# A decoder trunk whose first FFN takes x times the norm's weights, with the root put on its results, and whose last two column halves end in banks of their own

## The chip, the cores and the metric

The kernel runs on one core of one Trainium2 chip. The metric is the device time of one execution in microseconds, as the median of several runs. In profile lines PE is TensorE's matmuls, PEld its weight loads, DVE is VectorE, ACT is ScalarE, POOL is GpSimd and SP is SyncE, on whose queue nearly all DMAs are issued.

## The reference, cut to what matters

```
def rms_norm(x, g):
    y = x * rsqrt(mean(x * x, axis=-1) + 1e-6)
    return y * g

def swiglu(x, w_in, w_out):
    gate, up = split(x @ w_in, 2, axis=-1)
    return (silu(gate) * up) @ w_out

h = x                                           # (1, 256, 1024) float32
for layer in range(2):
    h = h + 0.5 * swiglu(rms_norm(h, ffn1_norm[layer]), ffn1_w_in[layer], ffn1_w_out[layer])   # 1024 -> 2 * 2816 -> 1024
    hn = rms_norm(h, mix_norm[layer])
    h = h + attention(hn)                       # layer 0: stick-breaking; layer 1: sliding window with sinks, shared K/V
    h = h + 0.5 * swiglu(rms_norm(h, ffn2_norm[layer]), ffn2_w_in[layer], ffn2_w_out[layer])
    # after layer 0: the shared K and V are computed from rms_norm(h, kv_norm) @ kv_w
return rms_norm(h, final_norm)
```

## The kernel before, in words

All 256 tokens are held in two tiles of 128 (t is 0 or 1); `hN` holds the stream, by tile and by halves of 512 columns (j is 0 or 1). Weights stream from HBM once, in pieces of 1 MB into five buffers `raw`. For accuracy each product is made of three: a weight is split into `w_hi` (cast on ACT, L362) and `w_lo` (difference on DVE, L364), the operand into `xh` and `xl` (both in the tile `xT`), and `step` does hi times hi, lo times hi and hi times lo into one PSUM bank, 512 columns wide.

An FFN (`ffn`) goes through its 2816 columns in blocks. The first block is `plain` (gate columns, then up columns), the second is `narrow` (256 columns of each), and four blocks are `strassen`: seven products instead of eight, with sums of operands (`operand_sums`, tiles `S_h` and `S_l`) and sums of weights (DVE, and DMAs that add, issued by POOL). `silu` and `mul` make `m` from gate and up, `turn` transposes it on PE (L579) and splits it into `aT_h` and `aT_l`, and `out` multiplies it with `w_out` into four banks, the accumulators of tile and half (`accs`). These banks hold, before the first `out`, the transposed operand, out of which `operand_sums` takes its differences; so the first output product has to wait until those have been read.

**The opening.** x comes in four DMAs of 256 KB (tile, half), the first weight in four DMAs of 256 KB (`cut` 4), all on SP's queue. The norm's 1024 weights come in as a tile of 128 by 8 (`gcols`); DVE spreads them over a diagonal (`diag`) and PE multiplies this with ones, so that every partition has all weights in two banks (`g0`). Per tile ACT squares the two halves with their sums (`sq`, L438), DVE adds them up (L442), POOL takes the power of -0.5 (L445, the root), DVE scales x by root and weights (`xs`, L468), PE transposes (L413), ACT casts (L419) and DVE subtracts (L420) into `xT`. PE meanwhile does 40 products of constants ("warm"), which have the lowest priority.

**The order of the work.** The program is a list of tasks, each with an engine, an estimated duration, a priority (the position `plan.pos` in PE's dense work, less a lead) and the buffers that it reads and writes. `Plan.order` simulates the engines with these estimates and issues the tasks in the order that comes out; on the chip each engine then runs its list in order. A changed estimate can so change the order on any engine.

**The sliding-window stage** (`sliding_window`, its inner function `heads`) handles eight pairs of heads. For each: scores (PE, `kT_s,qT`), row maxima (DVE, L1140), the exponentials with their sums (ACT, L1149 and L1156), the inverse and the scaling of `e` (DVE, L1163 to L1166), six transposes of `e` (PE, L1174), two copies `ws` out of PSUM (ACT, and DVE at L1180), and the product with the values (PE, `ws,v_s`). Between these PE does query steps (`w_hi,xT`, 256 wide, with the rotary operations `qr_t` and `qr` on DVE) and steps of the output projection (`w_hi,o_h`).

**The end.** The last FFN has `ending` set: its last products go tile by tile and half by half, and the very last step (t = 1, j = 1) is done in two groups of three products of 256 columns into the two halves of one bank. `last` adds the results to the stream (L1304), squares (ACT L1309, DVE L1312), adds up (L1319), takes the root (POOL L1321), multiplies with the last norm's weights (L1325) and scales: columns 0 to 640 on DVE (L1331), 640 to 1024 on ACT (L1334), each followed by its output DMA (L1336).

Of the kernel before, what the change touches and what calls it, by code (L numbers as in the profile page):

```python
# [53 lines left out]
MASK_FROM = 2  # L54
QORD = (('q', 0, 1), ('q', 0, 0), ('q', 1, 0), ('q', 2, 0), ('h', 0, 0), ('h', 0, 1), ('q', 1, 1), ('h', 1, 0), ('h', 1, 1), ('q', 2, 1), ('h', 2, 0), ('q', 3, 0), ('h', 2, 1), ('q', 3, 1), ('h', 3, 0), ('h', 3, 1))
# [111 lines left out]
def dve(n):  # L167
    return n / 0.96 + 70
# [11 lines left out]
def kernel(  # L180
# [76 lines left out]
    one = pool.tile([P, 1], F32, name="one")  # L257
# [63 lines left out]
    def dma(src, dst, nbytes, w, prio, r=()):  # L321
        T("SP", nbytes / (300.0 if prio < -8e5 else PLAIN), lambda: nc.sync.dma_start(out=dst(), in_=src), r=r, w=w, prio=prio)
# [164 lines left out]
    def operand_sums(accs):  # L487
# [16 lines left out]
        T("ACT", act(512), lambda: ACT.copy(out=s[1].ap, in_=a[1][0].ap), r=B(a[1][0]), w=B(s[1]))  # L504
# [36 lines left out]
    def ffn(w_in, w_out, acc, rest, finish, kv=None, blocks=BLOCKS, first=False, ending=False):  # L541
        wi, wo = by_k(w_in), by_k(w_out)
        ring = [banks[i] for i in rest[0:3]]
# [3 lines left out]
        outs = {}  # L547
# [8 lines left out]
        def make_sums():  # L556
            nonlocal SH, SL
            SH, SL = operand_sums(accs)
# [4 lines left out]
        def col(h, i, c, n=512):  # L563
            return wi[:, 4 * i:4 * i + 4, h * DFF + c:h * DFF + c + n]

        def silu(dst, src, r, w, n=512):
            T("ACT", act(n), lambda: ACT.activation(out=dst(), in_=src(), func=AF.Silu), r=r + [(consts, "tbl")], w=w)

        def mul(dst, a_, b_, r, w, n=512):
            T("DVE", dve(n), lambda: DVE.tensor_mul(out=dst(), in0=a_(), in1=b_()), r=r, w=w, lat=LAT["DVE"] + TM)  # L570
# [17 lines left out]
        def plain(n, c, by_t, cut=2):  # L588
# [15 lines left out]
            def after_gate(t, bank):  # L604
                ms[t] = m = STG.get([P, 512], F32, "m")
                silu(lambda: m.ap, lambda: bank.ap, B(bank), B(m))

            def after_up(t, bank):
                m = ms[t]
                mul(lambda: m.ap, lambda: m.ap, lambda: bank.ap, B(bank), B(m))  # L610
                turn(m, t, aT)
# [30 lines left out]
        def narrow(n, c, by_t):  # L642
# [5 lines left out]
            def part(t, i):  # L648
# [5 lines left out]
                if i == 1:  # L654
                    m = STG.get([P, 512], F32, "m")
                    silu(lambda: m.ap[:, 0:256], lambda: bs[t].ap[:, 0:256], B(bs[t]), B(m), 256)
                    mul(lambda: m.ap[:, 0:256], lambda: m.ap[:, 0:256], lambda: bs[t].ap[:, 256:512], B(bs[t]), B(m), 256)
                    turn(m, t, aT, 2)
# [5 lines left out]
        def strassen(n, c, between):  # L664
# [13 lines left out]
            def mul_less(dst, a_, b_, r, w):  # L678
                T("DVE", dve(512), lambda: DVE.scalar_tensor_tensor(out=dst(), in0=b_(), scalar=-1.0, in1=a_(), op0=ALU.mult, op1=ALU.mult),
                  r=r, w=w, lat=LAT["DVE"] + TM)  # L680
# [21 lines left out]
            silu(lambda: s1.ap, lambda: s1.ap, [], B(s1))  # L702
# [4 lines left out]
            mul_less(lambda: s1.ap, lambda: s1.ap, lambda: u2.ap, B(u2), B(s1))  # L707
# [9 lines left out]
            silu(lambda: m.ap, lambda: a.ap, B(a), B(m))  # L717
            mul_less(lambda: m.ap, lambda: m.ap, lambda: p5.ap, B(p5), B(m))
# [11 lines left out]
        def out_step(n, i, kk, w, t, j, cut=False):  # L730
            if cut:

                for c in range(2):
                    (sh, sl), keys = of_a(outs[n][0], t, 2 * i + kk)
                    hi, lo = w
                    bank, now = accs[t][j], slice(256 * c, 256 * c + 256)

                    def run(now=now, cols=slice(512 * j + 256 * c, 512 * j + 256 * c + 256)):
                        mm(bank.ap[:, now], sh(), hi.ap[:, kk, cols], False, False)
                        mm(bank.ap[:, now], sl(), hi.ap[:, kk, cols], False, False)  # L740
                        mm(bank.ap[:, now], sh(), lo.ap[:, kk, cols], False, True)
                    dense(3 * mmr(256), run, r=[(hi, kk), (lo, kk)] + keys + (B(bank) if c else []), w=[(bank, c)])
                return
# [36 lines left out]
        for t in range(NT):  # L780
            for js in ((0,), (1,)) if ending else ((0, 1),):
                for n, i, w in ends:
                    for kk in range(2):
                        for j in js:
                            if ending and t == js[-1] == kk == 1 and (n, i) == ends[-1][0:2]:
                                out_step(n, i, kk, w, t, j, True)
                            else:
# [264 lines left out]
    def sliding_window(w_q, w_o, p0, others_, finish):  # L1052
# [54 lines left out]
        def heads(g, i):  # L1107
# [29 lines left out]
            T("PE", 850 if ready else 1230, scores, r=[(qT, (g, t)) for t in range(NT)] + [(kT_s, t) for t in range(NT)] + MWIN, w=B(*z))  # L1137
# [29 lines left out]
            T("DVE", 300 + dve(512) + dve(256), inverse, r=[(SM, (n, par, t)) for par in range(2) for t in range(NT)] + [(ES, (n, par)) for par in range(2)],  # L1167
# [8 lines left out]
            T("PE", 620, turns, r=[(e, (par, t)) for par in range(2) for t in range(NT)] + ID, w=B(*z))  # L1176
# [13 lines left out]
            T("PE", 800, av, r=[(w, k) for k in range(2)] + [(v_s, t) for t in range(NT)], w=[(o, k) for k in range(i, 2)])  # L1190
# [189 lines left out]
```

## Time and profile before

| | |
|---|---|
| time, median of 3 runs | 921.87 us (921.62 to 922.02) |
| the profiled execution: time, span | 922.51 us, 920.7 us |
| mean granted TensorE clock | 0.998 |
| busy: PE, DVE, ACT, POOL | 910.0, 797.9, 613.0, 55.7 us |
| first dense product of the first FFN | starts at 12.42 us |
| last product | ends at 913.98 us |
| mean HBM traffic | 226 GB/s |

The profile is of one execution, which took 0.64 us more than the median of the runs. The span runs from the first to the last instruction, and 1.8 us lie around it. A busy PE is one whose matmuls are under way; matmuls are pipelined, so that one of 512 columns shows some 0.39 us while the next starts after 0.23.

### The profile page before, as it was taken

The page shows a single profiled execution, that of the slowest core. Times are in us where ns is not written, and L with a number is a line of the kernel's source. Part 1 is how long each engine was busy: PE and PEld are TensorE (multiplying, and loading weights), DVE is VectorE, ACT ScalarE, POOL GpSimd, SP SyncE. Part 2 cuts the span into 40 slices and gives each one's busy share as a digit, 9 for nine tenths or more (in the row PEclk, how much of TensorE's full clock was granted, in tenths as well). Part 3 has the DMA queues.
Part 4 walks back from the last instruction along what each step waited for, and adds up shares of the span by engine and source line. Part 5 has one row for each costly group of instructions (what it writes and reads, how often), then busy time and mean ns, then how long its engine had stood idle before and what let it go on. Part 6 is the DMA issues. An engine that isn't in the chain of part 4 may idle for free.

```text
span 920.7 us, 11926 instructions
## 1 busy us (share of the span) xinstructions
PE 910.0 (99%) x4499; PEld 753.2 (82%) x4499; DVE 797.9 (87%) x962; ACT 613.0 (67%) x870; POOL 55.7 (6%) x65
## 2 busy tenths in 40 slices
PE   9999999999999999999999999999999999999997
PEld 6888888888888888888888888888897788888885
DVE  7979998798876887999879789998788798799984
ACT  6657667577887647676656477676758575667662
POOL 1010101010000000010000001010000000011000
PEclk9999999999999999999999999999999999999999
DMA  9878999895943577999884579999853358699961
GB/s 313 317 181 247 287 282 252 291 230 157 309 163 126 162 216 197 250 290 288 261 311 184 160 189 266 303 281 260 270 169 116 92 172 239 187 243 303 277 201 46
DMA packets 101930, 209.19 MB, mean 227 GB/s; under 512 B 3952, under 2 KB 24944, under 8 KB 101872
## 3 DMA queue, kind: packets, MB, share of 16 engines
q1 hardware_dynamic: 83104, 171.53, 53.0%
q0 software_dynamic: 18480, 36.70, 23.9%
q8 instruction: 35, 0.57, 0.2%
q10 hardware_dynamic: 288, 0.20, 0.1%
q14 instruction: 23, 0.19, 0.1%
HBM read 207.37 MB, written 1.05 MB: 226 GB/s over the span
## 4 chain that ended last, share of the span: by engine, by line
PE 97%; DVE 1%; ACT 1%; DMA 0%; issue 0%; DVEq 0%; ACTq 0%
PE ps L240 93%; PE ps L579 2%; PE ps L413 1%; PE ps L1174 1%; ACT e L1149 0%; DMA gcols<-in_ffn_norm_dram 0%; DVE w_lo L364 0%; DVE e L1166 0%; PE ps L1099 0%; ACT xT L419 0%; DVE small L1140 0%; DVE hN L1304 0%; DVE diag L1238 0%; DVE xT L420 0%; DVE hg L1325 0%
## 5 line engine op out<-in xcount | busy, mean ns | idle before, releaser
L364 DVE TENSOR_TENSOR w_lo<-raw,w_hi 128x1024 fp32r<-128x1024 f32 x418 | 491.2, 1218 | 32.0 <-ACT w_hi L362 30.8
L362 ACT CAST w_hi<-raw 128x1024 fp32r<-128x1024 f32 x418 | 417.3, 1051 | 99.7 <-PE ps L240 57.9
L240 PE MATMUL ps<-w_hi,xT 128*128 128x512 f32 (+1 forms) x920 | 270.6, 378 | 0.0
L240 PEld LDWEIGHTS ps<-w_hi,xT 128*128 128x128 f32 x920 | 166.9, 188 | 30.3
L240 PE MATMUL ps<-w_lo,xT 128*128 128x512 f32 (+1 forms) x460 | 172.5, 375 | 0.0
L240 PE MATMUL ps<-w_hi,aT_h 128*128 128x512 f32 x353 | 140.5, 398 | 0.0
L240 PE MATMUL ps<-w_lo,aT_h 128*128 128x512 f32 x353 | 137.7, 390 | 0.0
L240 PE MATMUL ps<-w_hi,aT_l 128*128 128x512 f32 x353 | 137.3, 389 | 0.0
L240 PE MATMUL ps<-w_hi,S_h 128*128 128x512 f32 x272 | 106.6, 392 | 0.0
L240 PE MATMUL ps<-w_lo,S_h 128*128 128x512 f32 x272 | 106.0, 390 | 0.0
L240 PE MATMUL ps<-w_hi,S_l 128*128 128x512 f32 x272 | 105.9, 389 | 0.0
L240 PEld LDWEIGHTS ps<-w_lo,xT 128*128 128x128 f32 x460 | 86.6, 188 | 15.8
L524 DVE TENSOR_TENSOR raw<-raw 128x1024 f32<-128x1024 f32 x66 | 78.6, 1218 | 0.3
L240 PEld LDWEIGHTS ps<-w_lo,aT_h 128*128 128x128 f32 x353 | 66.2, 188 | 14.2
L240 PEld LDWEIGHTS ps<-w_hi,aT_l 128*128 128x128 f32 x353 | 66.4, 188 | 12.8
L240 PEld LDWEIGHTS ps<-w_hi,aT_h 128*128 128x128 f32 x353 | 66.3, 188 | 12.6
L529 POOL DMA_DIRECT2D raw<-in_ffn_w_in_dram x32 | 41.0, 1282 | 526.5 <-ACT w_hi L362 285.6
L240 PEld LDWEIGHTS ps<-w_lo,S_h 128*128 128x128 f32 x272 | 51.1, 188 | 10.7
L240 PEld LDWEIGHTS ps<-w_hi,S_h 128*128 128x128 f32 x272 | 51.1, 188 | 10.3
L240 PEld LDWEIGHTS ps<-w_hi,S_l 128*128 128x128 f32 x272 | 51.1, 188 | 10.3
L419 ACT CAST aT_h<-ps 128x512 fp32r<-128x512 f32 (+1 forms) x48 | 26.4, 550 | 47.1 <-PE ps L579 47.1
L240 PE MATMUL ps<-xT,w_hi 128*128 128x512 f32 (+1 forms) x136 | 47.2, 394 | 0.1
(168 smaller groups left out, 900.8 us busy)
## 6 DMA issues: line engine op xcount, KB each, us to landing
raw<-in_ffn_w_in_dram SPq DMA_DIRECT2D x76, 1024.0 KB, 7.6
raw<-in_ffn_w_out_dram SPq DMA_DIRECT2D x44, 1024.0 KB, 5.5
raw<-in_ffn_w_in_dram POOLq DMA_DIRECT2D x32, 1024.0 KB, 9.4
raw<-in_sb_w_qkv_dram SPq DMA_DIRECT2D x12, 1024.0 KB, 7.7
raw<-in_ffn_w_in_dram SPq DMA_DIRECT2D x16, 512.0 KB, 5.2
raw<-in_ffn_w_in_dram SPq DMA_DIRECT2D x16, 256.0 KB, 5.3
raw<-in_sb_w_o_dram SPq DMA_DIRECT2D x4, 1024.0 KB, 6.8
raw<-in_swa_w_q_dram SPq DMA_DIRECT2D x4, 1024.0 KB, 8.7
```

The lines of the kernel that those rows point to most:

```text
L240: PE.matmul(ps, lhsT=lhsT, rhs=rhs, start=start, stop=stop, skip_group_check=True)
L362: T("ACT", act(m), lambda sl=sl: ACT.copy(out=flat(hi)[:, sl], in_=flat(raw)[:, sl]), r=[(raw, i) for i in rs] + first, w=[(hi, i) for i i ...
L364: T("DVE", dve(m), lambda sl=sl: DVE.tensor_sub(out=flat(lo)[:, sl], in0=flat(raw)[:, sl], in1=flat(hi)[:, sl].bitcast(F32)), r=[(raw, i) ...
L413: PE.transpose(out=bank.ap[:, i * P:(i + 1) * P], in_=s, identity=ident)
L419: T("ACT", act(n), lambda: ACT.copy(out=hi[2](), in_=src()), r=B(bank), w=[hi[0:2]])
L524: T("DVE", dve(m), lambda sl=sl: DVE.tensor_add(out=flat(dst)[:, sl], in0=flat(dst)[:, sl], in1=flat(src)[:, sl]), r=[(src, k) for k in ks ...
L529: T("POOL", 1500, lambda: nc.gpsimd.dma_start(out=dst.ap, in_=src, accum_op=ALU.add), w=[(dst, 0), (dst, 1)], prio=plan.pos - LOADS, lat=5 ...
L579: PE.transpose(out=tr.ap[:, i * P:(i + 1) * P], in_=m.ap[:, i * P:(i + 1) * P], identity=ident)
L1174: PE.matmul(z[par].ap[:, i_ * P:(i_ + 1) * P], lhsT=e.ap[:, par * 384 + c:par * 384 + c + P], rhs=ident, start=i_ == 0, stop=True, is_tran ...
```

## The change

*First FFN.* x is no longer scaled before its transposes. `first_operand` transposes x itself, taking every fourth column of a half for one transpose, so that the norm's weights lie per partition and column of the transposes; DVE multiplies the bank with them in place; cast and subtraction follow. For this the rows of `w_in` are grouped as (half, partition, 4) (`wi4`), in all blocks of this FFN. The weights come in as 128 by 2 by 4, and `diag`, `one` and `g0` are gone. The root and its negative (`roots`) are put onto the results: as the scale of `silu` and as the scalar of `mul` and `mul_less`. The sums of operands now begin after the first SiLU (`WAITM`). The second tile's x is issued behind four pieces of the first weight instead of two (`X1`).

*Planned costs.* The estimates for DMAs at the opening and for four kinds of tasks of the sliding-window stage are changed, and so the order there.

*The end.* The last two steps of t = 1, j = 1 go by halves of 256 columns, each half into a bank of its own (`last_steps`, `ends_in`). `last` first adds what the old accumulator holds to the stream, and then each of the two banks. Columns 0 to 640 are scaled and sent in two parts of 320.

```
+X1 = 35
+POSX = (-20000.0, -6000.0)
+POSR = (-3000.0, -2000.0)
-        T("SP", nbytes / (300.0 if prio < -8e5 else PLAIN), ...
+        T("SP", nbytes / (283.0 if prio < -8.5e5 + 50 else 375.0 if prio < -8e5 else PLAIN), ...
...
+        wi4 = w_in.rearrange("(j p k) n -> p j k n", j=2, k=4)
-            return wi[:, 4 * i:4 * i + 4, h * DFF + c:h * DFF + c + n]
+            cs = slice(h * DFF + c, h * DFF + c + n)
+            return wi4[:, i, :, cs] if first else wi[:, 4 * i:4 * i + 4, cs]
...
+            if first:
+                T("ACT", act(n, True), lambda: ACT.activation(out=dst(), in_=src(), func=AF.Silu, scale=roots[t][0].ap), ...
...
+                T("DVE", dve(n), lambda: DVE.scalar_tensor_tensor(out=dst(), in0=b_(), scalar=roots[t][0].ap, in1=a_(), op0=ALU.mult, op1=ALU.mult),
...
+        def last_steps(n, i, w, t, j):
+            for c in range(2):
+                hi, lo = w
+                for kk in range(2):
+                    (sh, sl), keys = of_a(outs[n][0], t, 2 * i + kk)
+                    def run(c=c, kk=kk, sh=sh, sl=sl, cols=slice(512 * j + 256 * c, 512 * j + 256 * c + 256)):
+                        now = ends_in[c].ap[:, 0:256]
+                        mm(now, sh(), hi.ap[:, kk, cols], kk == 0, False)
+                        mm(now, sl(), hi.ap[:, kk, cols], False, False)
+                        mm(now, sh(), lo.ap[:, kk, cols], False, kk == 1)
...
-            T("PE", 850 if ready else 1230, scores, ...
+            T("PE", 950 if ready else 1280, scores, ...
-            T("DVE", 300 + dve(512) + dve(256), inverse, ...
+            T("DVE", 400 + dve(512) + dve(256), inverse, ...
-            T("PE", 620, turns, ...
+            T("PE", 670, turns, ...
-            T("PE", 800, av, ...
+            T("PE", 890, av, ...
...
-        dma(xs_[:, t, half(j)], ..., -8.5e5 + 15 if t else -9e5)
+        dma(xs_[:, t, half(j)], ..., -8.5e5 + X1 if t else -9e5)
...
+    def first_operand(t, j, bank):
+        transposes(bank, lambda: [hN.ap[:, t, half(j)].rearrange("p (q k) -> p k q", k=4)[:, k, :] for k in range(4)], [(hN, (t, j))])
+        T("DVE", dve(512), lambda: DVE.tensor_mul(
+            out=quarters(bank), in0=quarters(bank), in1=gin[:, j].unsqueeze(2).to_broadcast([P, 4, P])), r=B(gc), w=B(bank))
+        part_to(bank, ...)
...
-        plan.pos = (-20000.0, -6000.0)[t]
-        rstds[t] = root(t)
-        for j in range(2):
-            if t == 0 and j == 1:
-                plan.pos = -6500.0
-            normed(t, rstds[t], g0, ring_pair((A0, A1)[t]), xh, xl, (j,))
+        plan.pos = POSX[t]
+        for j in range(2):
+            first_operand(t, j, banks[(A0, A1)[t][j]])
+        plan.pos = POSR[t]
+        r, minus = root(t), tiny(1)
+        roots.append((r, minus))
...
+            if t == n == 1:
+                add(pair[1], slice(0, 512), half(1), [], (hN, (1, 3)))
+            if t == 1 and n:
+                add(ends_in[n - 1], slice(0, 256), c, [(hN, (1, 3))], (hN, (t, n)))
```

SP's queue at the opening, before: `hN` is x, `raw` with 128x512 a piece of the first weight.

```order
L322 DMA hN<-in_x_dram 128x512 x2
L322 DMA raw<-in_ffn_w_in_dram 128x512 x2
L322 DMA hN<-in_x_dram 128x512 x2
L322 DMA raw<-in_ffn_w_in_dram 128x512 x14
L322 DMA raw<-in_ffn_w_in_dram 128x4x256 x2
```

And now:

```order
L326 DMA hN<-in_x_dram 128x512 x2
L326 DMA raw<-in_ffn_w_in_dram 128x512 x4
L326 DMA hN<-in_x_dram 128x512 x2
L326 DMA raw<-in_ffn_w_in_dram 128x512 x12
L326 DMA raw<-in_ffn_w_in_dram 128x4x256 x2
```

The second pair of x, which is the second tile, moved from the fifth and sixth place to the seventh and eighth.

PE where the first products of the FFN begin, before (behind 38 of the 40 warm-ups; `ident,xs` are four transposes of the second tile):

```order
L240 MATMUL ps<-w_hi,xT 128x512 x2
L240 MATMUL ps<-w_lo,xT 128x512
L413 MATMUL ps<-ident,xs 128x128 x4
L240 LDWEIGHTS warm
L240 MATMUL ps<-warm 128x256
```

And now, where the last of the 40 warm-ups ends (`ident,hN` are the transposes of the second tile's x):

```order
L245 MATMUL ps<-warm 128x256
L417 MATMUL ps<-ident,hN 128x128 x4
L245 MATMUL ps<-w_hi,xT 128x512 x2
L245 MATMUL ps<-w_lo,xT 128x512
L417 MATMUL ps<-ident,hN 128x128 x4
```

All warm-ups and the first four transposes of the second tile now stand ahead of the first product. The first tile's transposes moved forward: behind 12 and 14 warm-ups, where they stood behind 24 and 26 and the broadcast; 26 warm-ups follow them.

DVE in the sliding-window stage, around the scaling of `e` for the third pair of heads, before:

```order
L1009 TENSOR_TENSOR qr_t<-ps,rp 128x4x32
L1010 TENSOR_TENSOR qr_t<-ps,rp 128x4x32
L1011 TENSOR_TENSOR qr<-ps,rp 128x256
L1163 TENSOR_TENSOR small<-small 128x2x2
L1164 RECIPROCAL small<-small 128x2x2
L1166 TENSOR_TENSOR e<-e,small 128x2x256
L1166 TENSOR_TENSOR e<-e,small 128x2x128
L1012 TENSOR_TENSOR qr<-qr,qr_t 128x256
L364 TENSOR_TENSOR w_lo<-raw,w_hi 128x1024
L1180 COPY ws<-ps 128x384
```

And now:

```order
L1182 TENSOR_TENSOR small<-small 128x2x2
L1183 RECIPROCAL small<-small 128x2x2
L1185 TENSOR_TENSOR e<-e,small 128x2x256
L1185 TENSOR_TENSOR e<-e,small 128x2x128
L1028 TENSOR_TENSOR qr_t<-ps,rp 128x4x32
L1029 TENSOR_TENSOR qr_t<-ps,rp 128x4x32
L1030 TENSOR_TENSOR qr<-ps,rp 128x256
L1031 TENSOR_TENSOR qr<-qr,qr_t 128x256
L1199 COPY ws<-ps 128x384
```

The rotary operations moved behind the scaling of `e`, and the `w_lo` there moved to a later place. On PE, the transposes of this pair now follow three more query steps; those of the first pair are followed by one query step ahead of its values product, where five stood; and those of the last pair follow two output steps instead of one.

137 lines of the change are left out of this document (66 added, 71 removed).

## The prediction

> **What bounds the kernel now.** I read the chain of waits first, then busy time by stretches, then the opening, the sliding-window stage and the end as timelines.
>
> ```profile
> span 920.7 us, 11926 instructions
> ...
> PE 97%; DVE 1%; ACT 1%; DMA 0%; issue 0%; DVEq 0%; ACTq 0%
> ```
>
> The chain is TensorE (PE) for 97% of the span. So a change pays where PE starts late, waits, or has finished. Columns below: stretch in us, its length, then busy us of PE, PEld, DVE, ACT, POOL with counts, granted clock, DMA share, GB/s.
>
> ```profile
> 12.40:60.00 47.60, 47.60 (x223) 39.31 (x221) 42.68 (x49) 30.34 (x40) 1.43 (x1) 1.00 0.90 292
> 60.00:182.00 122.00, 122.00 (x556) 100.96 (x556) 110.41 (x112) 83.32 (x100) 9.49 (x8) 1.00 0.94 266
> ...
> 695.00:700.00 5.00, 4.01 (x30) 3.37 (x27) 4.90 (x13) 4.69 (x22) 0.00 (x0) 1.00 0.54 210
> ...
> 720.00:730.00 10.00, 8.84 (x53) 6.71 (x52) 6.93 (x16) 5.14 (x16) 0.00 (x0) 1.00 0.36 105
> ...
> 914.00:921.00 7.00, 0.00 (x0) 0.00 (x0) 2.62 (x8) 1.13 (x3) 0.55 (x1) 0.75 0.20 75
> ```
>
> In the first FFN (12.4 to 182) PE never pauses, while DVE still has 5 of 47.6 us and 12 of 122 us free. PE loses about 2 us in the sliding-window stage, and 7 us after its last matmul. The opening is the fourth place:
>
> ```profile
> 0.93 3.17 PE L240 MATMUL ps<-warm 128*128 128x256 bf16 x14 [0.93 <-DVE warm L271]
> ...
> 3.88 0.63 ACT L438 ACTIVATE sq<-hN 128x512 bf16<-128x512 f32 x1 [1.42 <-DMA hN<-in_x_dram]
> ...
> 4.80 3.78 PE L240 MATMUL ps<-diag,one 128*128 128x512 f32 x4 [0.69 <-DVE diag L1238]
> ...
> 7.89 1.04 ACT L362 CAST w_hi<-raw 128x1024 fp32r<-128x1024 f32 x1 [2.54 <-DMA raw<-in_ffn_w_in_dram]
> ...
> 9.28 1.22 DVE L364 TENSOR_TENSOR w_lo<-raw,w_hi 128x1024 fp32r<-128x1024 f32 x1
> ...
> 9.62 0.61 PE L240 MATMUL ps<-warm 128*128 128x256 bf16 x4
> ...
> 11.16 1.50 PE L240 MATMUL ps<-warm 128*128 128x256 bf16 x12
> ...
> 11.32 1.35 DVE L420 TENSOR_TENSOR xT<-ps,xT 128x512 fp32r<-128x512 f32 x2 [0.75 <-ACT xT L419]
> ...
> 12.42 0.71 PE L240 MATMUL ps<-w_hi,xT 128*128 128x512 f32 x2
> ```
>
> The first weight piece is ready at 10.5 (9.28 + 1.22), the first operand's lower part only at 12.0 (half of 1.35 after 11.32), and the first product begins at 12.42, after twelve more warm-ups. From the chain of waits:
>
> ```profile
> 15.84 21.14 PE ps L240 x93
> ...
> 36.98 0.44 PE ps L579 x4
> ```
>
> A product takes 21.14 / 93 = 0.227 us, a step (three) 0.682. Up to 36.98 PE's order has 34 steps and two sets of four transposes at 0.44: 23.2 + 0.9 = 24.1. Run without a break this work would have begun at 36.98 - 24.1 = 12.9. That is the number which the change has to beat.
>
> **The opening, part by part.** *Removed:* the broadcast of the norm's weights (two diag products, two DVE builds) and the four scaled copies xs. *Added:* four DVE multiplications of 512 columns in PSUM and two tiny negations. DVE's count of 512-wide operations there falls by two; nothing of this is paid by PE.
>
> *Moved: x before its root.* The first half of x has landed at 3.88 (row of ACT), so its transposes can go at about 3.9 instead of 10.1. One first-tile half then needs transposes, multiplication, ACT cast and DVE subtraction; both halves need some 3 us of DVE at 0.68 each, so the first tile is ready near 7.5, before its weights (10.2: cast 7.89 + 1.04, then 1.22 on a DVE that is now free). The weights and the second tile decide the start.
>
> *Moved on SP's queue:* the second tile's x goes behind four weight pieces, not two. What a place in that queue is worth:
>
> ```profile
> L322 SPq DMA_DIRECT2D raw<-in_ffn_w_in_dram x2: 432/432/433, 1.6 to 2.1; - x2
> ...
> DMA to landing us min/median/max: 3.6/4.6/5.7
> L322 SPq DMA_DIRECT2D hN<-in_x_dram x1: 432/432/432, 3.1 to 3.1; - x1
> ...
> DMA to landing us min/median/max: 6.1/6.1/6.1
> L322 SPq DMA_DIRECT2D raw<-in_ffn_w_in_dram x1: 432/432/432, 3.6 to 3.6; - x1
> ...
> DMA to landing us min/median/max: 6.3/6.3/6.3
> ```
>
> The pieces are all 256 KB, issued at 1.65, 2.12, ... 3.56; they land at 5.25, 7.8, ... 9.2 (sixth) and 9.86 (seventh), from 7.8 on about 0.68 apart. The seventh place is now x of the second tile: 9.86, its next half 10.5. In PE's order its transposes stand ahead of the first product, so PE cannot begin before about 9.9. The weight pieces behind come no later than PE needs them: 0.68 each, four for 5.5 us of PE.
>
> *The warm-ups.* All forty still stand ahead of the first product: 12, transposes, 2, transposes, then 26. At first one takes 0.21 us (14 in 3.17, with the last one's tail), later 0.105 (twelve from 11.16 to 12.42); by the row at 9.62 the rate has doubled, with the granted clock at 1.00 in all rows. The change-over lies at about 9.5. Transposes at the slow rate take twice 0.44. So: 3.9 + 0.88 + 0.42 + 0.88 = 6.0 is when the 26 begin. If the rate doubles at 9.5 again, 16 run slow and 10 fast: 6.0 + 3.5 + 1.05 = 10.5. Bounds: 9.9 (rate up early, x decides) and 11.5 (26 x 0.21, rate never up). I take 10.5, since that is the change-over that the trace shows. The gain at the opening is 12.9 - 10.5 = 2.4, between 0.5 and 3.0.
>
> The Trainium skill ("TensorE: Matmul & The Clock Gate", Part 1) says the array runs at half rate until a free-running window of about 3.4 us has been busy, and (Part 4) that transposes do not count as busy. The trace agrees on the doubling (0.21 to 0.105); by this rule the window after 6.0 could close as late as 12.9, which is the second rival below.
>
> *Strided transposes.* They now read every fourth column of x; no row shows such a read. Bounds: nothing, or twice the 0.44 for the two sets of the second tile, 0.9. I take nothing, as nearest to the rows of plain transposes, and keep 0.9 for the range. The Trainium skill ("SBUF — State Buffer", the remark on 16-byte cachelines under "Door 1") speaks against the change here: full rate needs two hits in a line, and this read has one. It gives no price; with a doubling the sum would be 0.9 later.
>
> *Sums of operands, root on the results.* The sums (copies and differences for the Strassen blocks) come after the gate's SiLU instead of before. Their banks are wanted by the first output product: at 10.5 + 0.9 + 48 steps + 0.9 = 45. DVE has, from the first up result at about 30, five w_lo at 1.22 and nine 512-wide operations at 0.68: 12.2, done by 42.3. Cover 2.7 us; if it went, PE would wait at that bank. The SiLU with the root as scale and the product with it as scalar lie on ACT and DVE, which have 17 and 5 us free in the first row above: nothing. The weights' rows are read in another order with the same 2 KB runs: nothing, or at worst the opening's gain (third rival).
>
> Does the gain last? In the first FFN nothing but PE's own rate holds PE back, and DVE would have to do 153 us of work in 167 instead of 170: yes.
>
> **The sliding-window stage.** Only planned costs are changed there, which moves rows.
>
> ```profile
> PE ps L1174 <- ACT small L1156: 1.0, 1, 1.0
> ...
> PE ps L1174 <- DVE e L1166: 0.7, 1, 0.7
> ...
> PE ps L240 <- ACT o_h L1200: 0.5, 1, 0.5
> ```
>
> ```profile
> 687.62 1.22 DVE L364 TENSOR_TENSOR w_lo<-raw,w_hi 128x1024 fp32r<-128x1024 f32 x1
> 688.76 0.55 DVE L1180 COPY ws<-ps 128x384 f32<-128x384 f32 x1
> ...
> 690.41 0.87 PE L240 MATMUL ps<-ws,v_s 128*64 128x256 f32 x8
> ...
> 696.70 0.28 DVE L1009 TENSOR_TENSOR qr_t<-ps,rp 128x128 f32<-128x128 f32 x1
> ...
> 697.43 0.15 DVE L1163 TENSOR_TENSOR small<-small 128x4 f32<-128x4 f32 x1
> ...
> 697.83 1.03 DVE L1166 TENSOR_TENSOR e<-e,small 128x512 f32<-128x512 f32 x2
> ```
>
> The wait of 1.0 (the turn of the third pair of heads) ends really with DVE's e at 698.9. Three rotary operations (696.70 to 697.43, 0.7) now come behind e, and three query steps more stand ahead on PE: that wait goes. The one of 0.7 gets one more output step (0.68) ahead: it goes too. Together -1.7. Against it: the first values product now follows its transposes by one query step where five stood (before, it came 1.1 after ws was ready at 689.3), and w_lo still lies ahead of ws on DVE. PE gets there about 0.7 before ws; the next turn waits for e some 0.4, and one later values product has a second w_lo ahead, 0.3. Net -0.3; bounds -1.7 (the two waits go, nothing new) and +1.
>
> **The end.**
>
> ```profile
> 913.70 0.28 PE L240 MATMUL ps<-w_lo,aT_h 128*128 128x256 f32 x1
> ...
> 914.01 0.76 DVE L1304 SCALAR_TENSOR_TENSOR hN<-ps,hN 128x256 f32<-128x256 f32 x2 [3.77 <-PE ps L240]
> ...
> 914.80 0.43 DVE L1312 SCALAR_TENSOR_TENSOR sq<-hN 128x256 f32<-128x256 f32 x1
> ...
> 916.99 0.36 ACTq L1336 DMA_DIRECT2D out_dram<-hg  x1
> ```
>
> Both additions run after the last product (913.98), though the first half's was done some 0.35 earlier: same bank. Now the first half ends six products of 256 columns (0.12 each) before the last, in its own bank; a third addition of 512 columns (0.68) takes in the old sums while PE works. One addition is left behind PE, 0.38 saved. PE's work grows by nothing (twelve of 0.117 for six and three of 0.227). The output in halves of 320 is not last, ACT's part is. Bounds 0 and 0.76; I take 0.4.
>
> **Sum.** -2.4 - 0.3 - 0.4 = -3.1. The profiled execution took 922.51 (span 920.7 and 1.8 around it): 919.4. The median of the runs is 0.64 below it: 921.87 - 3.1 = 918.8.
>
> **Rivals.** *More:* x decides the start (9.9, gain 3.0), the waits of 1.7 go with no new ones, the end gives 0.76: 921.87 - 5.5 = 916.4.
> *The rate doubles late:* 26 slow warm-ups to 11.5, then slow transposes (0.44 more) and a first slow step or so: work begins as if at 12.4, gain 0.5, and 921.87 - 0.5 - 0.7 = 920.7. For it: little but transposes and slow warm-ups runs before 6. Against: today the change-over comes 4.7 us after the pause at 4.8.
> *The opening moves nothing:* if the interleaved weight rows land slower by the 2.5 us that one piece (5.25 to 7.8) already shows, the weights decide at 12.9: 921.2.
> *Slower:* if in the sliding-window stage all eight values products come one step behind their transposes and wait the 0.7, that is 5.6 against 2.8 gained elsewhere: 924.7. It decides from 0.58 per product; only one of eight is moved so near.
>
> **How the numbers follow.** A measurement of this kernel tells about 0.2% from no change (1.84 us). Forecast 0.56 (own range 917.4 to 920.0); more 0.15; rate late 0.12; opening moves nothing 0.10; slower 0.07. Faster: 0.56 + 0.15 and a little of the late rate, 0.73. Within: 0.20. Slower: 0.07. The range 916.8 to 921.3 leaves out the slower case and the far ends of two others.
>
> **What would show it.** First step near 10.5 and not 12.4, and the first output product's transposes 2.4 earlier; no PE pause before 182; PE's waits at the turns of e below 1.7 in sum; from the last product to the last DVE scaling 0.4 less. I would be wrong if PE pauses at the first output product (sums late), if x of the second tile lands well after 9.9, or if new waits for ws appear.

## The result: 917.16 us, and the profile after

The changed kernel takes 917.16 us (median of 6 runs, 916.41 to 917.56); the kernel before took 921.54 on the same chip (6 runs). The ratio is 0.9949, 95% interval 0.9939 to 0.9960: 4.4 us less, where 3.1 less was forecast (the forecast of 918.8 started from the earlier median of 921.87). The profiled execution took 917.11, its span 915.3, so the spans differ by 5.4. That is 1.0 more than the medians do, and the reason turns out below to be a property of the opening before.

The page of the kernel after, its first line and the line of the chain by engine:

```profile
span 915.3 us, 11921 instructions
...
PE 98%; DMA 1%; DVE 0%; ACT 0%; SPq 0%; issue 0%; DVEq 0%; ACTq 0%
```

TensorE (PE) carries the chain still, so the time that went must show as a lead of PE's order. The opening as a timeline (start in us, length, engine and line, operation, in brackets the idle time ahead and what ended it):

```profile
0.93 2.74 PE L245 MATMUL ps<-warm 128*128 128x256 bf16 x12 [0.93 <-DVE warm L275]
...
3.69 1.10 PE L417 MATMUL ps<-ident,hN 128*128 128x128 f32 x4
...
4.96 0.63 PE L417 MATMUL ps<-ident,hN 128*128 128x128 f32 x4
...
5.43 3.08 PE L245 MATMUL ps<-warm 128*128 128x256 bf16 x26
...
7.93 1.23 DVE L368 TENSOR_TENSOR w_lo<-raw,w_hi 128x1024 fp32r<-128x1024 f32 x1
...
9.14 0.75 PE L417 MATMUL ps<-ident,hN 128*128 128x128 f32 x4 [0.63 <-DMA hN<-in_x_dram]
...
9.64 0.71 PE L245 MATMUL ps<-w_hi,xT 128*128 128x512 f32 x2
...
10.43 0.63 PE L417 MATMUL ps<-ident,hN 128*128 128x128 f32 x4
...
10.81 0.70 PE L245 MATMUL ps<-w_hi,xT 128*128 128x512 f32 x2
```

The 26 warm-ups take 3.08 us with the last one's tail, about 0.11 each: the rate had doubled before them, between the first set of transposes (1.10) and the second (0.63). PE is through with them at 8.5, waits 0.63 for x of the second tile, and begins at 9.14; the first w_lo is ready at 9.16. From the chain of waits of the kernel after, the first output product's transposes:

```profile
32.85 0.44 PE ps L594 x4
```

Ahead of them stand 33 steps (one of before's 34 now comes later) and two sets: 32.85 - 33 x 0.682 - 0.88 = 9.46. Against 12.9 before, the opening is worth 3.45. PE never waits from there to 182.

The sliding-window stage, from the transposes that stand ahead of it to those of the next FFN's operand; from the chain of waits of before, then of after:

```profile
660.53 0.44 PE ps L413 x4
...
735.40 0.44 PE ps L413 x4
```

```profile
657.05 0.44 PE ps L417 x4
...
730.32 0.44 PE ps L417 x4
```

74.87 became 73.27: 1.60 less. Of the three waits of PE there, one is left, by the list of waits of after:

```profile
PE ps L245 <- ACT o_h L1219: 0.5, 1, 0.5
```

The end of the kernel after:

```profile
908.67 0.28 PE L245 MATMUL ps<-w_lo,aT_h 128*128 128x256 f32 x1
...
908.99 0.42 DVE L1317 SCALAR_TENSOR_TENSOR hN<-ps,hN 128x256 f32<-128x256 f32 x1 [0.21 <-PE ps L245]
...
909.45 0.42 DVE L1334 SCALAR_TENSOR_TENSOR sq<-hN 128x256 f32<-128x256 f32 x1
...
910.00 0.22 DVE L1341 SCALAR_TENSOR_TENSOR small<-small 128x1 f32<-128x1 f32 x1
...
910.40 0.76 DVE L1347 TENSOR_TENSOR hg<-hN,gain 128x128 f32<-128x128 f32 x2 [0.18 <-issue]
...
911.90 0.39 ACTq L1360 DMA_DIRECT2D out_dram<-hg  x1
```

One addition stands behind the last product instead of two, and sq begins 0.50 after that product's end (908.95), where it took 0.82. But hg then starts late, with nothing named for 0.18, and ACT's output DMA goes out 2.95 after the product's end, against 3.01 before. The span ends 6.35 after it, against 6.72: 0.37 less. In sum 3.45 + 1.60 + 0.37 = 5.4, the difference of the spans.

### The profile page after: what moved, and what is told of

Read it like the earlier page. It is cut to its first block, busy times and chain, and to the rows that moved or that the text cites. A ratio compares the mean times of both kernels' runs of the same rounds, so it can differ in the third digit from the quotient of the medians.

```text
span 915.3 us, 11921 instructions
## 1 busy us (share of the span) xinstructions
PE 906.8 (99%) x4498; PEld 752.7 (82%) x4498; DVE 798.3 (87%) x964; ACT 614.5 (67%) x870; POOL 55.1 (6%) x65
## 4 chain that ended last, share of the span: by engine, by line
PE 98%; DMA 1%; DVE 0%; ACT 0%; SPq 0%; issue 0%; DVEq 0%; ACTq 0%
PE ps L245 94%; PE ps L594 2%; PE ps L417 1%; PE ps L1193 1%; DMA hN<-in_x_dram 1%; SPq L326 0%; PE ps L1118 0%; ACT xT L423 0%; DVE hg L1347 0%; DVE xT L424 0%; ACT hg L1358 0%; ACT s L508 0%; DVE sq L1334 0%; DVE hN L1317 0%; ACT o_h L1219 0%
## 5 line engine op out<-in xcount | busy, mean ns | idle before, releaser
L245 PEld LDWEIGHTS ps<-w_lo,xT 128*128 128x128 f32 x460 | 86.5, 188 | 15.8
L245 PEld LDWEIGHTS ps<-w_lo,S_h 128*128 128x128 f32 x272 | 51.1, 188 | 10.8
L245 PEld LDWEIGHTS ps<-w_hi,S_h 128*128 128x128 f32 x272 | 51.1, 188 | 10.5 <-ACT p L688 0.2
L245 PEld LDWEIGHTS ps<-w_hi,S_l 128*128 128x128 f32 x272 | 51.1, 188 | 10.2
```

The costliest lines, as they stand in the source:

```text
L245: PE.matmul(ps, lhsT=lhsT, rhs=rhs, start=start, stop=stop, skip_group_check=True)
```

## Experiments: the parts by themselves

The three parts of the change share no instruction: each alone gives, on every engine, the new order in its own stretch and the old one elsewhere. Three kernels have one part each. A fourth asks what sets the start: it is the changed kernel without the 26 warm-ups.

**The opening alone** (all of the diff but its lines on the sliding window and on the end).

> The kernel before with the opening alone changed (norm's weights on the transposes, root on the results, x of the second tile behind four pieces, its DMA rates in the plan); sliding window and end as before. In the two profiled executions the first output product's transposes moved 3.4 us ahead, against 2.4 predicted. Theory A: the opening is worth 3.4 in every execution, so 921.5 - 3.4 = 918.1. Theory B: one of those executions is off by about 1 us in its opening (the kernel before's ran 0.6 to 1.0 above its median), and the opening is worth 2.4: 919.1. In the trace: PE's first step at about 9.6, no pause before 182, PE's waits of 1.0 and 0.7 in the sliding window still there.

Measured 919.16 (7 runs) against 922.04 (23 runs of the kernel before, beside it): ratio 0.9971, interval 0.9960 to 0.9982, that is 1.7 to 3.7 less. The median lies at theory B's value; the trace shows theory A's lead again (first output transposes at 32.65). Both are true if the kernel before does not always begin as in its profile, and the third kernel shows that it does not.

**The sliding window alone.**

```diff
-            T("PE", 850 if ready else 1230, scores, ...
+            T("PE", 950 if ready else 1280, scores, ...
-            T("DVE", 300 + dve(512) + dve(256), inverse, ...
+            T("DVE", 400 + dve(512) + dve(256), inverse, ...
-            T("PE", 620, turns, ...
+            T("PE", 670, turns, ...
-            T("PE", 800, av, ...
+            T("PE", 890, av, ...
```

> The kernel before with only the planned costs of the sliding-window stage changed. Theory A (the traces: that stage got 1.65 us shorter): 921.5 - 1.65 = 919.9, PE idle in the stage down from 2.1 (without the last wait) to 0.4, the waits of 1.0 and 0.7 gone, and one values product of 1.33 in place of 0.87 us, which is its wait for ws. Rival (as predicted: 1.7 gone, new waits of 0.7, 0.4 and 0.3): 921.5 - 0.3 = 921.2.

920.20 (11 runs): ratio 0.9981, interval 0.9972 to 0.9990, 1.8 less. The stage takes 73.28 us in its trace (660.72 to 734.00), 1.6 less, and the waits of 1.0 and 0.7 are gone. The rival is out.

**The end alone.**

```diff
+                        now = ends_in[c].ap[:, 0:256]
...
+                add(pair[1], slice(0, 512), half(1), [], (hN, (1, 3)))
...
+                add(ends_in[n - 1], slice(0, 256), c, [(hN, (1, 3))], (hN, (t, n)))
...
-        for j, c in enumerate(cuts):
+        for j, c, ks in ((0, slice(0, 320), (0,)), (1, cuts[1], (640,)), (0, slice(320, 640), (0, 512))):
```

> The kernel before with only the end changed (halves in own banks, output of the first 640 columns in two DMAs). Theory A: 0.35 less from the last product to the end of the span (6.70 to 6.35 in the traces): 921.2. Rival: the issue of the last DMA moved by only 0.06, the rest is the scatter of a DMA's landing, and the time stays at 921.5. Second rival: the full 0.76 of an addition, 920.8.

921.27 (11 runs): ratio 0.9993, interval 0.9985 to 1.0002, so by time the edit cannot be told from nothing. The trace tells more. Its end, from the addition behind the last product (which ended at 912.84):

```profile
912.88 0.42 DVE L1304 SCALAR_TENSOR_TENSOR hN<-ps,hN 128x256 f32<-128x256 f32 x1 [0.21 <-PE ps L240]
...
914.02 0.76 DVE L1334 TENSOR_TENSOR hg<-hN,gain 128x128 f32<-128x128 f32 x2
...
915.52 0.38 ACTq L1347 DMA_DIRECT2D out_dram<-hg  x1
```

Here hg starts without the pause, ACT's DMA goes out 2.68 after the product (0.33 less than before; the DMA of columns 320 to 640, on SP's queue, goes out 0.1 after it), and the span of 919.0 ends 6.16 after the product. So the edit is worth 0.33 up to ACT's DMA, and some 0.2 more behind it: from that issue to the end of the span it is 3.4 to 3.6 in the kernels with the new end, 3.7 to 3.8 in those with the old one. In the kernel after, the pause ahead of hg takes 0.27 of it back.

The opening of this kernel is that of the kernel before, instruction for instruction. In its trace:

```profile
0.93 3.04 PE L240 MATMUL ps<-warm 128*128 128x256 bf16 x14 [0.93 <-DVE warm L271]
4.55 1.98 PE L240 MATMUL ps<-diag,one 128*128 128x512 f32 x4 [0.57 <-DVE diag L1240]
```

```profile
35.77 0.44 PE ps L579 x4
```

The four broadcast products took 1.98 us and not 3.78, and the first output transposes came at 35.77 and not 36.98. The norm's weights had landed 0.25 sooner, PE's pause ahead of those products was 0.57 and not 0.69, and the rate had doubled before it. So the opening before has an early and a late course, 1.2 us apart. One series of its runs looks like them: of 15, 7 lie at 920.6 to 921.5 and 8 at 922.1 to 923.0. The 23 runs beside this kernel fill 920.8 to 922.8 without such a gap, so the groups alone would not have shown it. The profiled execution of the kernel before (922.51) took the late course, and the opening's gain is 3.45 against that one, and 35.77 - 32.85 - 0.68 = 2.2 against the other.

**Few warm-ups.**

```diff
-        T("PE", 450 if i < 8 else 245, lambda n=2: warm_up(n), ...
+        T("PE", 450 if i < 8 else 245, lambda n=2 if i < 7 else 0: warm_up(n), ...
```

> The changed kernel without the 26 warm-up products behind the second set of transposes (14 are left ahead of it). Theory A: x of the second tile (9.1) and the first weights' lower part (9.15) set the start, the 26 warm-ups end at 8.5 and set nothing; without them the start stays at 9.1, and the time at 917.2, unless the pause of 3.6 us lets TensorE fall back to its slow rate, when the first steps would take twice their 0.68 us for some 3 us: 918 to 920. Rival (as predicted: the warm-ups decide): the start moves ahead by as much as they took, 916.

918.49 (5 runs), ratio 0.9968, 0.9956 to 0.9981: 1.3 above the changed kernel's 917.16, which was measured apart from it. Its trace:

```profile
5.18 0.63 PE L417 MATMUL ps<-ident,hN 128*128 128x128 f32 x4
9.01 1.13 PE L417 MATMUL ps<-ident,hN 128*128 128x128 f32 x4 [3.19 <-DMA hN<-in_x_dram]
9.79 1.20 PE L245 MATMUL ps<-w_hi,xT 128*128 128x512 f32 x2
...
11.93 0.70 PE L245 MATMUL ps<-w_hi,xT 128*128 128x512 f32 x2
```

Transposes and products fell back to half rate in the pause of 3.2 us and had the full rate again at about 11.9, 2.9 us after PE began again. The start stayed at 9.0: the warm-ups set nothing by their length, x and the weights do. What the warm-ups buy is the rate at 9.0, some 1.1 us (first output transposes at 33.98, not 32.85).

## Experiments: when the rate doubles

**The kernel before, without its pause.**

```diff
-        T("PE", 450 if i < 8 else 245, lambda n=2: warm_up(n), ...
+        T("PE", 450 if i < 8 else 245, lambda n=3 if i < 7 else 2: warm_up(n), ...
```

> The kernel before with 21 warm-up products instead of 14 ahead of the broadcast of the norm's weights, so that PE has no pause between 4.1 and 4.8. Theory A: the pause of 0.6 to 0.7 us there decides whether TensorE's rate doubles at about 4 or only at 8.5 to 10. With no pause it doubles at 4 to 5 in every execution, the four broadcast products take 1.9 us and not 3.8, the first output product's transposes begin at about 35.8 and not 37.0, and the runs, which for the kernel before reach from 920.8 to 922.8, lie together near 921.0. Rival: the moment of doubling is chance, or the weights decide: 922.0, as before.

```profile
0.93 4.66 PE L240 MATMUL ps<-warm 128*128 128x256 bf16 x21 [0.93 <-DVE warm L271]
5.38 2.60 PE L240 MATMUL ps<-diag,one 128*128 128x512 f32 x4
```

First output transposes at 35.85, as theory A said. The broadcast products took 2.60, between its 1.9 and 3.78: the rate doubled during the second of them, at about 6.8, and not at 4 to 5 as theory A had it. So without a pause it still does not double at one moment. The runs reach from 920.72 to 921.88 (11 runs), while the kernel before reached from 920.63 to 922.98 beside them: the upper group is gone, the lower one is not beaten. By the medians (921.51 against 922.08; ratio 0.9996, interval 0.9987 to 1.0005) no gain is shown; the spread is what changed.

**The changed kernel, with a pause put in.**

```diff
-        T("PE", 450 if i < 8 else 245, lambda n=2: warm_up(n), ...
+        T("PE", 450 if i < 8 else 245, lambda n=0 if 3 <= i < 6 else 2: warm_up(n), ...
```

> The changed kernel with six warm-up products fewer at the very start, so that PE stands still from about 2.3 to 3.7, and all else the same. Theory A: such a pause takes the early doubling of TensorE's rate away: the 26 warm-ups behind the second set run at 0.21 for longer, the rate doubles at 7 to 10.5 and not at 4.9, the start slips from 9.1 to between 9.3 and 11, and the runs spread over 917.2 to 919 with a median of 918 or more. Rival: the doubling depends on what runs after 3.7 alone, and the second tile's x decides the start: 917.2.

918.76 (5 runs, 917.69 to 919.50), 1.6 above the changed kernel's 917.16; ratio 0.9965, 0.9952 to 0.9977. Theory A holds in the median and in the trace, though two of the five runs took 917.7:

```profile
0.93 1.46 PE L245 MATMUL ps<-warm 128*128 128x256 bf16 x6 [0.93 <-DVE warm L275]
3.89 1.10 PE L417 MATMUL ps<-ident,hN 128*128 128x128 f32 x4 [1.50 <-DMA hN<-in_x_dram]
...
6.06 4.45 PE L245 MATMUL ps<-warm 128*128 128x256 bf16 x26
10.35 0.64 PE L417 MATMUL ps<-ident,hN 128*128 128x128 f32 x4
```

The same 26 warm-ups take 4.45 and not 3.08, 13 or 14 of them slow (the rate doubles at about 9.0), and the second tile's transposes go at 10.35, when x has been there since 9.4 at the latest (ACT reads it then). This is what I had predicted of the changed kernel itself (start at 10.5 behind slow warm-ups), and it needs a pause to come true.

The Trainium skill ("TensorE: Matmul & The Clock Gate", Part 1) says that the window over which activity is counted is about 3.4 us long and runs freely, so that the moment of doubling varies from run to run. The traces agree that it varies. Without a pause after 0.93 the full rate came at about 4.8 in the changed kernel, at about 6.4 in two others whose PE order is the same there (one is the kernel with two memsets more, further below, whose first two or three of the 26 are slow), and at about 6.8 in the kernel before with 21 warm-ups. After the pause of 0.67 in the kernel with the sliding window alone, which ended at 4.76, seven or eight of the next ten warm-ups are slow, and it came at about 9.9. In the kernel with few warm-ups it came 2.9 us after PE began again, so PE had not been busy throughout a window of 3.4. The warm-ups with the two memsets, then those with the sliding window alone:

```profile
5.83 3.32 PE L245 MATMUL ps<-warm 128*128 128x256 bf16 x26
```

```profile
8.34 2.05 PE L240 MATMUL ps<-warm 128*128 128x256 bf16 x10
...
10.22 0.60 PE L413 MATMUL ps<-ident,xs 128*128 128x128 f32 x4
```

Over all fourteen traces, by the length of PE's pause behind the first warm-ups: the nine with none or at most 0.38 have the full rate by 6.8 at the latest, the four with 0.65 to 1.50 only at 9.0 to 9.9. The one with 0.57 (the end alone) had it by 4.6, so where the border lies is open.

## Experiments: stride, weights, and what binds next

**Columns and rows in the old order**, twice; the order of all engines is the same.

```diff
-            return wi4[:, i, :, cs] if first else wi[:, 4 * i:4 * i + 4, cs]
+            return wi[:, 4 * i:4 * i + 4, cs]
...
-        transposes(bank, lambda: [hN.ap[:, t, half(j)].rearrange("p (q k) -> p k q", k=4)[:, k, :] ...
+        transposes(bank, lambda: [hN.ap[:, t, half(j)][:, k * P:(k + 1) * P] ...
...
-    ... nc.scalar.dma_start(out=gin, in_=ffn1_norm[0].rearrange("(j p k) -> p j k", j=2, k=4)) ...
+    ... nc.scalar.dma_start(out=gin, in_=ffn1_norm[0].rearrange("(j k p) -> p j k", j=2, k=4)) ...
```

> The changed kernel with x's columns, the weights' rows and the norm's weights in the order of before (the transposes read 128 columns in a row; each partition's row of a weight is 128 rows from the next); the order of all engines is the same. Theory A: the stride costs nothing (a set of four transposes 0.44 to 0.47 either way) and the weights land no sooner or later: 917.2. Rival: the stride costs up to 0.9 in the four sets, so 916.3. Second rival: the weights' interleaved rows are why the first cast began at 6.85 and not at 7.89: 917.7 to 918.2.

918.29 (5 runs, 917.67 to 919.63): neither theory's 917.2 nor the gain of the first rival; the second rival's 917.7 to 918.2 is near, but not for its reason. The trace, of the slowest of the five, has the pause again, ahead of the first transposes, since x landed late:

```profile
4.33 1.09 PE L417 MATMUL ps<-ident,hN 128*128 128x128 f32 x4 [0.65 <-DMA hN<-in_x_dram]
...
6.49 4.68 PE L245 MATMUL ps<-warm 128*128 128x256 bf16 x26
```

The third line pair is why this test was not clean: in the old order the norm's weights come in 1024 pieces of 4 bytes, ahead of x. So it was run without that pair.

> The changed kernel with x's columns and the weights' rows in the order of before, while the norm's weights are still fetched in pieces of 16 bytes (they then fall on columns they don't belong to, which changes the output and no duration). It splits the miss of the kernel in which these were fetched in pieces of 4 bytes (918.3; x's first half landed at 4.2 there against 3.6 to 3.9). Theory A: the 4-byte pieces delayed x, the delay opened a pause on PE, and with it TensorE's rate doubled late; now 917.2, x's first half at 3.6 to 3.9, a set of four transposes some 0.04 shorter than the strided one. Rival: the weights' rows 128 apart land later, 918.3 again.

917.18 (5 runs, 916.51 to 917.48), ratio 0.9948, 0.9936 to 0.9961: theory A. The slowest of these runs is below the quickest of the ones with the 4-byte fetch, so that fetch costs about 1.1 us in the medians, and the weights' order nothing. (In the trace above 1.7 is lost up to the first output transposes, at 34.53, and 0.7 more at 86 us, of which below.) The stride's price stands in the starts of a set of transposes and of what follows it:

```profile
10.13 0.60 PE L417 MATMUL ps<-ident,hN 128*128 128x128 f32 x4
10.48 0.71 PE L245 MATMUL ps<-w_hi,xT 128*128 128x512 f32 x2
```

0.35 for a plain set; 0.38 (10.43 to 10.81, shown above) for a strided one. By the cacheline remark of the Trainium skill ("SBUF — State Buffer", under "Door 1") that read should fall short of full rate. The trace agrees, and gives the price: 0.03 to 0.04 a set, some 10%, not the doubling that I had kept as an end of the range.

**x of the second tile two places further ahead.**

```diff
-X1 = 35
+X1 = 15
```

> The changed kernel with the second tile's x behind two weight pieces, as it was before, instead of four. If x's landing alone decides the start, PE's steps begin at 9.2 with both sets of transposes done, 1.1 sooner: 916.1. Theory A: the first weight's second half then lands some 1.3 later (at 9.9), its lower part is ready at 11 to 12.2, and PE waits for it after two steps: 917.2 to 918.

917.17 (5 runs, ratio 0.9950, 0.9937 to 0.9962). Both expectations missed. The steps began at 9.99 with all transposes done, not at 9.2: the first w_lo was ready only at 9.71, as its cast began at 7.39 and not at 6.85, and four warm-ups stood last ahead of the step.

```profile
8.48 1.23 DVE L368 TENSOR_TENSOR w_lo<-raw,w_hi 128x1024 fp32r<-128x1024 f32 x1
```

And PE did not wait for the first weight's second half, since the plan had put two of the second tile's steps ahead of it. First output transposes at 32.88: the same work in another order, and the same end.

**The very first weight in four pieces.**

```diff
+        hi.fine = raw.cut == 4 and not splits
...
-            rs = [2 * j, 2 * j + 1] if raw.cut == 4 else ks
+            rs = [j] if hi.fine else [2 * j, 2 * j + 1] if raw.cut == 4 else ks
...
-        piece = kk // 2 if piece is None else piece
+        piece = (kk if getattr(hi, "fine", False) else kk // 2) if piece is None else piece
```

> The changed kernel with the very first weight cast and split in four operations of 512 columns each instead of two of 1024, so that a step waits for one row of blocks and not for two. Theory A (x of the second tile at 9.1 and the first w_lo at 9.15 share the start): the first w_lo is ready at 8.2 to 8.6 instead, the first step begins there, ahead of the second tile's transposes, and the second tile's operand (12.5 to 12.8) becomes the next limit: the first output transposes move by 0.3 to 0.6, 916.7. Rival: x of the second tile alone decides, 917.2.

917.34 (5 runs, ratio 0.9952, 0.9940 to 0.9965). The first step began at 7.45, and the first output transposes came 0.5 sooner than in the changed kernel, as theory A had it. At the end of this FFN only 0.18 of that was left (the long run of products behind it starts at 193.37, not 193.55). The rest goes at 86 us, where three other kernels that start 0.2 to 0.4 sooner lose theirs too, and more. From the kernel of the next paragraph, ACT's row there and the list of waits of PE:

```profile
84.69 2.00 ACT L369 CAST w_hi<-raw 128x1024 fp32r<-128x1024 f32 x2 [1.19 <-DMA raw<-in_ffn_w_in_dram]
```

```profile
PE ps L245 <- ACT p L691: 0.5, 1, 0.5
```

A weight of 1 MB, fetched over POOL's queue, lands 10.8 to 11.3 us after its issue in these four traces, and its cast begins at 84.0 to 84.7; behind that cast stands the copy p that PE needs at about 86.5. In the changed kernel the same transfer took 10.5, the cast began at 84.16, and PE did not wait. But the lead does not decide it: the opening alone starts 0.2 sooner, its transfer took 10.2, and it keeps its lead (193.35); the kernel with the 4-byte fetch starts 1.7 later, its transfer took 11.2, and PE waits 0.4 all the same. Why this transfer takes 10.2 in one trace and 11.3 in another was not tried.

**Two more instructions on DVE**, and the same with 16 warm-ups ahead of the first transposes instead of 12.

```diff
+    spare = pool.tile([P, 2], F32, name="spare")
+    for i in range(2):
+        T("DVE", 60, lambda i=i: DVE.memset(spare[:, i:i + 1], 0.0), prio=-8e5)
```

> The changed kernel with two more tiny memsets on DVE at the start, nothing else. At the end of the changed kernel DVE's hg starts 0.18 us later than its operands allow, with nothing named, and so it does in two other kernels with the same DVE order; in one with two more DVE instructions ahead it does not. Theory A: the pause hangs on the number of the instruction in DVE's order (its supply of instructions). Then two more ahead move it away from the end: hg starts 0.14 after the small sum and not 0.40, and from the last product's end to the last DMA issue it is 2.68 and not 2.95. Rival: the pause is of this place in the program (its operands, its neighbours): 2.95 again.

```profile
910.86 0.22 DVE L1344 SCALAR_TENSOR_TENSOR small<-small 128x1 f32<-128x1 f32 x1
910.99 0.76 DVE L1350 TENSOR_TENSOR hg<-hN,gain 128x128 f32<-128x128 f32 x2
...
912.49 0.39 ACTq L1363 DMA_DIRECT2D out_dram<-hg  x1
```

The last product ended at 909.81: hg starts 0.13 after the small sum, and ACT's DMA goes out at 2.68. Theory A, to the number. The kernel with x two places further ahead supports it: on its DVE one more wait for a semaphore stands ahead of the end, and the pause stands one instruction earlier, ahead of the small sum.

```profile
910.39 0.22 DVE L1341 SCALAR_TENSOR_TENSOR small<-small 128x1 f32<-128x1 f32 x1 [0.47 <-DVE sq L1334]
```

Elsewhere that sum follows sq after 0.12. The time of the single run with the memsets, 917.74, is not lower, for this kernel waited 0.5 at 86 us.

```diff
-        T("PE", 450 if i < 8 else 245, lambda n=2: warm_up(n), ...
+        T("PE", 450 if i < 8 else 245, lambda n=3 if i < 4 else 2 if i < 18 else 0: warm_up(n), ...
```

> The changed kernel with the two memsets on DVE and with 16 warm-up products in place of 12 ahead of the first transposes (40 in all, as it was). If x's first half lands late, PE then has no pause ahead of them. Theory A: rate doubled by 5 in every execution, and 0.27 less at the end: 916.9, with no run above 917.4. Rival: no difference that can be told, 917.2.

918.04 (5 runs, 916.78 to 918.20), ratio 0.9954, 0.9940 to 0.9967: the expectation failed. The rate doubled by 5 and the end was short, as meant (2.68), but its trace shows two waits that the changed kernel hasn't: 0.4 for p in the first FFN, and 0.2 for a DVE result in the last one (at 840.6). Its runs lie in two groups (916.8 to 917.1 and 918.0 to 918.2), and the trace is of the upper one with an early doubling: two groups need not come from the rate. No version beat the changed kernel by more than the measurement can tell.

## Why the prediction was right, and where its terms were not

The sign and the range held: 917.16 against 918.8, range 916.8 to 921.3. It lies just below the forecast's own range (917.4 to 920.0), and nearer to the rival *More* (916.4) than to the forecast. Two of the three gains were larger than forecast, and the third came out near its number by luck; the range was wide enough. Point by point:

- *The opening, -2.4.* In the profiled executions 3.45, a little over the bound of 3.0; alone, by medians, 2.9 (1.7 to 3.7). The step that failed is the change-over of the rate at 9.5. I took it from the trace of before as a time on the clock, but there it was the consequence of a pause of 0.69 us; without one it came at about 4.8, and the warm-ups (0.11 each at the full rate, not 0.105) were done at 8.5, not 10.5. The sentence "if the rate doubles at 9.5 again" named the assumption; the bound beside it ("rate up early, x decides") was the true case, with x at 9.1 and not 9.9.
- *Weights and second tile decide the start; sums covered; strided transposes nothing.* These held: x at 9.10 and w_lo at 9.16, no pause of PE before 182, 0.03 to 0.04 a set.
- *The gain lasts.* It did, but with little to spare: four kernels that start 0.2 to 0.5 sooner lose that, in part or whole, at 86 us.
- *The sliding window, -0.3.* 1.60 in two traces. The removed waits (1.7) were right; the mis-sized term is what would take their place, 1.4 in sum. A new wait for ws, which the prediction had named as a sign of being wrong, did come, but alone. Rows of after, DVE and PE:

```profile
684.01 1.22 DVE L368 TENSOR_TENSOR w_lo<-raw,w_hi 128x1024 fp32r<-128x1024 f32 x1
685.14 0.55 DVE L1199 COPY ws<-ps 128x384 f32<-128x384 f32 x1
...
686.01 1.03 DVE L1185 TENSOR_TENSOR e<-e,small 128x512 f32<-128x512 f32 x2
```

```profile
685.28 1.33 PE L245 MATMUL ps<-ws,v_s 128*64 128x256 f32 x8
...
687.09 0.87 PE L1193 MATMUL ps<-ident,e 128*128 128x128 f32 x6
```

  The values product took 1.33 instead of 0.87: the wait for ws is there, inside its row, 0.46 and not 0.7, as its first half needs only what ACT had copied. Delayed by that, PE reaches the next turn when e is ready (687.04), so the 0.4 did not come on top: two waits in a row on one engine are not added. The 0.3 did not come either (ws ready at 700.30, PE there at 700.7). One wait I had not seen went as well: in the trace before, the first turn starts at 687.85, 0.24 later than its predecessor's products would let it, as e is ready at 687.70. 1.7 + 0.24 - 0.46 = 1.5 of the 1.6; the last 0.1 is not assigned.
- *The end, -0.4.* 0.37 of the span, but not by the step that I had: 0.33 came up to ACT's DMA and 0.27 of it was lost again to the pause ahead of hg; the rest lies behind that issue, which I had costed at nothing. The sign that the prediction named did not come: the last DVE scaling ends 2.81 after the last product in both kernels (916.24 + 0.55 before, 911.08 + 0.68 now).

Of the rivals, *More* was nearly the case (x decides, the waits go), without the 0.76 at the end. *The rate doubles late* is real, and showed in the kernels with a pause (918.8, 918.3), not in this one. *The opening moves nothing* and *slower* are out: the weights' rows cost nothing in either order, and one product of eight waited.

## What to carry to other kernels

A time at which TensorE's rate doubles, read from one trace, is not a constant of the kernel: look for pauses of PE ahead of it and for a spread of the runs, and keep PE busy from the start without a pause until its first real work. Waits that a reordering creates one behind the other on the same engine overlap and are not to be summed, while waits shorter than the profile lists hide in rows that are longer than their kind. Before paying for an earlier start, look for the next transfer or engine that arrives just in time; here 0.3 of another 0.5 us was gone at 86 us.

## What was not expected of the hardware

- A pause of PE of 0.57 us at 4 us left the doubling of the rate early (full rate by 4.6, end alone); pauses of 0.65 to 0.69 went with a doubling at 9.5 to 9.9 (kernel before, sliding window alone, 4-byte fetch). A pause of 3.2 us brought half rate back for some 2.9 us.
- DVE stands still for 0.17 to 0.18 us ahead of the same instruction in five kernels with the same DVE order, and not there in four with one or two more DVE operations ahead of it. In a sixth, with one more wait for a semaphore, it stands one instruction earlier. It goes by the place in DVE's stream of instructions. The Trainium skill ("Runtime: NRT & Kernel Launch", Instruction fetch mechanics) says that instructions are fetched in blocks and that crossing into the next is mostly hidden; that this pause is such a crossing was not tried.
- A fetch of 4 KB in 4-byte pieces instead of 16-byte ones at the very start costs about 1.1 us of the whole (medians). In the one trace x lands at 4.2, and a pause and a late doubling follow; part of that trace's loss comes at 86 us, and is not shown to hang on the fetch.
